# Layer A of a two-layer decoder step: an odd unit's scores and transposes in two visits of four banks, and the short chunk's scores beside the first transposes

## The chip, the cores and the metric

One core of one Trainium2 chip. The metric is device time in microseconds (us) of one execution. The kernel is one launch that computes the whole step; its program is laid out in advance, engine by engine: TensorE (PE), VectorE (DVE), ScalarE (ACT), GpSimd (POOL) and SyncE (SP), which issues nearly all DMAs.

## The reference, cut to what matters

Layer 0 is an RWKV-7 time mixing over 272 prompt tokens (16 meta tokens and 256 of the prompt) and 8 sample tokens, with 64 heads of 64. Four projections of width 4096 (r, k, v, z) feed a recurrence per head:

```python
def rwkv7_step(S, inp):
    r, d, k, v, kk, b = inp
    sa = jnp.einsum('bhij,bhj->bhi', S, kk)
    S = S * d[:, :, None, :] - sa[..., None] * b[:, :, None, :] + v[..., None] * k[:, :, None, :]
    return S, jnp.einsum('bhij,bhj->bhi', S, r)
```

Its output is normalised per head, gated with silu(z) and projected back. Layer 1 is a sliding-window attention; the change doesn't touch it.

## The kernel before, in words

**Large products.** The projections are 128x128 matmuls over 280 columns. Weights are split in two fp32r parts (`whi` by ACT at L195, `wlo` by DVE at L197), so each 128-row step takes three matmuls (L218, L219, L220). Layer A has 64 such products of 16 *pieces* each; a piece is six matmuls.

**The recurrence in chunks.** The prompt is cut in four chunks of 64 tokens and a short one of 16. A *unit* `u` is two pairs of heads, that is four heads; there are 16 units, and two of them (even, odd) make a group `o` of eight heads. For each unit `prep` and `prep_e` make `KB` (keys, one buffer for all units) and `E` (queries). Then `scores(u)` does three things:
- scores of chunks 0 and 1, of chunks 2 and 3 (`c0` 0 and 2; L1013, 8 matmuls each), and of the short chunk (L1027, 4 matmuls), each into two PSUM banks, one for each `q`. They use 64 rows and 128 columns of the array. In the profile an f32 matmul has two records, so a visit of 8 shows as x16.
- ACT copies the blocks of the triangular system out of the banks into `F` and `ND` (L1019, L1032), and DVE writes masked scores into `E` (L1020, L1021, L1033, L1034).
- transposes of `KB` for the two head pairs `j` (L1045, 10 each, one record each), which ACT copies to `BK` (L1047).

After the short chunk's scores of an odd unit, `substitute(o)` inverts the 16x16 triangular blocks of the whole group, mostly on DVE: POOL masks `ND`, a transpose to `NL` (L1065), 28 small steps in sequence (L1071, L1073), and transposes to `TN` and `TR` (L1077, L1078). `solve(o)` (L1098 to L1128, matmuls `ps_so`) joins the blocks, and `chain(o)` (matmuls `ps_ch`) runs the five chunks. `group_norm` transposes the result (`ps_yt`, L1271, read by DVE at L1272).

**What sets the order.** `drive` takes one piece of a large product, then lets every stream whose time has come put its matmuls behind it, and so on. A stream says with `yield n` how many pieces it waits before its next step; one such step is called a *visit* here. On PE this order is kept as written; DVE and ACT are ordered by a scheduler that is run when the program is built. An even unit's scores run as a side stream beside the chain of the group before; an odd unit's are part of the stream `main`: scores, `solve`, `chain`, and so on for eight groups.

**Banks.** `pm` (3 banks) takes the large products, `pe` (2 banks) the scores, the transposes and `solve`, `pp` (1) small work, and `pcy` (one tile of two banks, `two_banks`) the chain and `group_norm`. Before, an odd unit's second and fourth visits borrow `pcy` as well.

## Time and profile before

| | |
|---|---|
| three runs | median 2121.87 us (2119.55 to 2125.27) |
| profiled execution | 2132.89 us, of which span 2131.1 us |
| TensorE clock granted, mean | 0.989 |
| busy, share of the span | PE 97%, DVE 79%, ACT 59%, POOL 6% |
| from 150 to 1290 us (layer A's recurrence beside its products) | 1140 us: PE busy 1099.99, DVE 879.85, ACT 738.48 |

The profile is one execution, 11 us above the median of the runs. Times in it are counted from the span's start. "Busy" of PE counts matmuls that overlap in the array, so a busy PE can still lose time between matmuls; that is read from the starts of neighbouring matmuls.

### The profile page before, as it was taken

What the parts mean: (1) busy time and instruction counts of PE and PEld (TensorE: products, weight loads), DVE (VectorE), ACT (ScalarE), POOL (GpSimd) and SP (SyncE); (2) the same over time, 40 slices, a digit from 0 to 9 for tenths busy, and PEclk for the clock granted to TensorE, in tenths of its full rate; (3) what the DMA queues carried; (4) which work ended last, traced back from release to release, by engine and by line L of the source; (5) the groups of instructions that cost most, each with busy time, mean ns of one, the idle gap of its engine ahead of it and who ended that gap; (6) DMA issues with size and microseconds to landing.
All of it is one profiled execution on the core that took longest, in us unless ns stands there. A gap on an engine that the chain in (4) does not pass through costs nothing.

```text
span 2131.1 us, 55813 instructions
## 1 busy us (share of the span) xinstructions
PE 2073.1 (97%) x21420; PEld 1971.4 (93%) x21420; DVE 1685.4 (79%) x4080; ACT 1252.9 (59%) x2757; POOL 121.5 (6%) x188
## 2 busy tenths in 40 slices
PE   9999999899999989999999999999999999999997
PEld 7999898899899989999999999999999999999997
DVE  7866767687678768888888787987888888878885
ACT  3456666576765757767675455565565655644443
POOL 0011100001010010100100001100000000000000
PEclk9999999999999999999999999999999999999999
DMA  7997667668657766777656678757455454567774
GB/s 256 315 314 243 177 215 241 183 186 289 208 178 211 251 207 204 214 225 212 203 161 222 217 239 253 237 186 223 143 149 171 137 158 135 178 203 252 227 220 134
DMA packets 276356, 446.28 MB, mean 209 GB/s; under 512 B 54056, under 2 KB 97768, under 8 KB 275696
## 3 DMA queue, kind: packets, MB, share of 16 engines
q1 hardware_dynamic: 275656, 441.66, 66.4%
q8 instruction: 168, 2.75, 0.5%
q10 hardware_dynamic: 432, 1.05, 0.1%
q14 instruction: 100, 0.82, 0.1%
HBM read 381.69 MB, written 65.03 MB: 210 GB/s over the span
## 4 chain that ended last, share of the span: by engine, by line
PE 60%; DVE 3%; DMA 2%; issue 1%; ACT 1%; POOL 0%; POOLq 0%; DVEq 0%; SPq 0%; ACTq 0%
PE ps_z L218 6%; PE ps_z L219 5%; PE ps_z L220 5%; PE ps_ob L218 3%; PE ps_ob L220 3%; PE ps_ob L219 3%; PE ps_q L218 3%; PE ps_q L220 3%; PE ps_q L219 3%; PE ps_oa L219 2%; PE ps_oa L218 2%; PE ps_oa L220 2%; PE ps_o L218 1%; PE ps_o L219 1%; PE ps_o L220 1%
## 5 line engine op out<-in xcount | busy, mean ns | idle before, releaser
L218 PE MATMUL ps_z<-mhlm,whi_z 128*128 128x280 f32 x512 | 158.7, 310 | 0.4 <-ACT st L789 0.4
L220 PE MATMUL ps_z<-mhlm,wlo_z 128*128 128x280 f32 x512 | 149.6, 292 | 2.7 <-issue 2.7
L218 PE MATMUL ps_q<-bmh,whi_qb 128*128 128x264 f32 x512 | 150.0, 293 | 0.4 <-ACT whi_qb L195 0.3
L219 PE MATMUL ps_z<-mhlm,whi_z 128*128 128x280 f32 x512 | 149.8, 292 | 0.0
L218 PE MATMUL ps_z<-bmh,whi_zb 128*128 128x264 f32 x512 | 147.5, 288 | 0.0
L220 PE MATMUL ps_q<-bmh,wlo_qb 128*128 128x264 f32 x512 | 145.6, 284 | 0.6 <-DVE wlo_qb L197 0.6
L219 PE MATMUL ps_q<-bml,whi_qb 128*128 128x264 f32 x512 | 145.6, 284 | 0.0
L219 PE MATMUL ps_z<-bml,whi_zb 128*128 128x264 f32 x512 | 145.4, 284 | 0.0
L220 PE MATMUL ps_z<-bmh,wlo_zb 128*128 128x264 f32 x512 | 145.4, 284 | 0.0
L218 PE MATMUL ps_ob<-ghi,whi_ob 128*128 128x264 f32 x512 | 145.3, 285 | 0.0
L220 PE MATMUL ps_ob<-ghi,wlo_ob 128*128 128x264 f32 x512 | 144.6, 284 | 0.0
L219 PE MATMUL ps_ob<-glo,whi_ob 128*128 128x264 f32 x512 | 144.6, 283 | 0.0
L195 ACT CAST whi_ob<-raw_ob 128x512 fp32r<-128x512 f32 x128 | 79.1, 620 | 96.9 <-PE ps_ob L219 75.4
L195 ACT CAST whi_oa<-raw_oa 128x512 fp32r<-128x512 f32 x128 | 79.2, 620 | 89.7 <-PE ps_oa L219 27.9
L197 DVE TENSOR_TENSOR wlo_r<-raw_r,whi_r 128x512 fp32r<-128x512 f32 x128 | 87.5, 688 | 48.7 <-ACT whi_r L195 46.3
L218 PE MATMUL ps_v<-mhlm,whi_v 128*128 128x280 f32 x384 | 121.4, 316 | 0.4 <-ACT st L789 0.4
L218 PE MATMUL ps_k<-mhlm,whi_k 128*128 128x280 f32 x384 | 120.4, 313 | 1.1 <-ACT st L789 1.1
L197 DVE TENSOR_TENSOR wlo_v<-raw_v,whi_v 128x512 fp32r<-128x512 f32 x128 | 87.4, 687 | 41.0 <-ACT whi_v L195 37.8
L195 ACT CAST whi_v<-raw_v 128x512 fp32r<-128x512 f32 x128 | 79.1, 618 | 66.5 <-PE ps_v L219 39.5
L195 ACT CAST whi_zb<-raw_zb 128x512 fp32r<-128x512 f32 x128 | 78.2, 619 | 62.6 <-PE ps_z L219 39.3
L220 PE MATMUL ps_k<-mhlm,wlo_k 128*128 128x280 f32 x384 | 112.9, 294 | 1.2 <-issue 1.1
L219 PE MATMUL ps_k<-mhlm,whi_k 128*128 128x280 f32 x384 | 113.0, 294 | 0.0
(473 smaller groups left out, 7584.2 us busy)
## 6 DMA issues: line engine op xcount, KB each, us to landing
raw_k<-a_w_rkvz SPq DMA_DIRECT2D x128, 256.0 KB
raw_v<-a_w_rkvz SPq DMA_DIRECT2D x128, 256.0 KB
raw_r<-a_w_rkvz SPq DMA_DIRECT2D x128, 256.0 KB
raw_z<-a_w_rkvz SPq DMA_DIRECT2D x128, 256.0 KB
raw_oa<-a_w_out SPq DMA_DIRECT2D x128, 256.0 KB
raw_qb<-b_w_qz SPq DMA_DIRECT2D x128, 256.0 KB
raw_zb<-b_w_qz SPq DMA_DIRECT2D x128, 256.0 KB
raw_ob<-b_w_o SPq DMA_DIRECT2D x128, 256.0 KB
```

Of the source, the lines that this page charges most:

```text
L195: self.nc.scalar.copy(hi, src)
L197: return self.nc.vector.tensor_tensor(lo, src, hi.bitcast(F32), op=ALU.subtract)
L218: mm(ps, wh, xh, start=start, stop=False)
L219: mm(ps, wh, xl, start=False, stop=False)
L220: return mm(ps, wl, xh, start=False, stop=stop)
```

## The change

Visits of a unit's scores and transposes, with the pieces waited before each:

| | before | after |
|---|---|---|
| even unit | 8 c0=0; 6 c0=2; 6 short chunk; 5 transposes j=0; 4 transposes j=1 | 8 c0=0; 6 c0=2; 6 short chunk and transposes j=0; 5 transposes j=1 |
| odd unit | 8 c0=0; 3 c0=2; 4 short chunk; 3 transposes j=0; 3 transposes j=1 | 8 c0=0 and c0=2; 8 short chunk, transposes j=0 and j=1 |

The short chunk's scores take columns 0 to 63 of their two banks, and the transposes of j=0 columns 64 to 383 of the same banks. In an odd unit the second part of each visit goes to `pcy`. The copies out of the banks stand behind the whole visit; `substitute` comes behind the short chunk's copies and ahead of those of the transposes. `solve` then waits 30 pieces where it waited 24 behind the last transposes (33 and 27 from group 5 on). No matmul, copy or DMA is added or removed.

```diff
-        gap = iter((8, 3, 4, 3, 3) if odd else (8, 6, 6, 5, 4))
-        turn = iter((0, odd, 0, odd, 0))
-        def banks(nm):
-            if next(turn):
+        gap = iter((8, 8) if odd else (8, 6, 6, 5))
+        def banks(second, nm):
+            if second and odd:
...
+        def pairs(ps, c0):
+            for j in range(2):
+                for c in range(2):
+                    for q in (1, 0):
+                        o = 64 * (c0 + c)
+                        mm(ps[q][:, j, c], kb(q, j, c0 + c), rows(q, j, o, o + 64), start=True, stop=True)
...
+        def last(ps):
             for j in range(2):
                 for q in (1, 0):
+                    mm(ps[q][:, j], kb(q, j, 4), rows(q, j, 256, L), start=True, stop=True)
...
+        def turned(ps, j):
+            for c in range(5):
+                for q in (1, 0):
+                    transpose(ps[q][:, c], kb(q, j, c), self.ident[H(q), H(q)])
+
+        def turned_out(ps, j):
             for q in range(2):
                 A.copy(BK[:, j, :, H(q)], ps[q])
+
+        for c0 in (0, 2):
+            if c0 == 0 or not odd:
+                yield next(gap)
+            ps = [b.rearrange("p (a c t) -> p a c t", a=2, c=2) for b in banks(c0, f"sc{c0}_{u}")]
+            with self.pe_order():
+                pairs(ps, c0)
+            if odd:
+                two = [ps] if c0 == 0 else [*two, ps]
+            else:
+                pairs_out(ps, c0)
+        if odd:
+            for i in range(2):
+                pairs_out(two[i], 2 * i)
+
+        yield next(gap)
+        bs = banks(0, f"sc4_{u}")
+        ps = [b[:, :64].rearrange("p (a h t) -> p a h t", a=2, h=2) for b in bs]
+        bk = [[b[:, 64:384].rearrange("p (c t) -> p c t", c=5) for b in bs]]
+        with self.pe_order():
+            last(ps)
+            turned(bk[0], 0)
+        if not odd:
+            last_out(ps)
+            turned_out(bk[0], 0)
+            yield next(gap)
+        bk.append([b[:, :320].rearrange("p (c t) -> p c t", c=5) for b in banks(1, f"bk{u}")])
+        with self.pe_order():
+            turned(bk[1], 1)
+        if odd:
+            last_out(ps)
+            self.substitute(u // 2)
+            turned_out(bk[0], 0)
+        turned_out(bk[1], 1)
...
-        yield 24 if o < 5 else 27
+        yield 30 if o < 5 else 33
```

`pairs_out` and `last_out` hold the same ACT copies and DVE masks as before, in functions.

In the order rows below, names are line, operation, output and inputs, and the size of the output. Place one is PE in odd unit 7, where the scores of chunks 0 and 1 end (`ps_sc10_7`, `ps_sc00_7` before; `ps_sc0_71`, `ps_sc0_70` after). Before:

```order
L1013 MATMUL ps_sc10_7_9357<-E_7_9230,KB_1737 128x128
L1013 MATMUL ps_sc00_7_9356<-E_7_9230,KB_1737 128x128
L218 MATMUL ps_r_2560_1_9337<-mhlm0_23_0_8424,whi_r_2560_0_9293 128x280
L219 MATMUL ps_r_2560_1_9337<-mhlm0_23_0_8424,whi_r_2560_0_9293 128x280
L220 MATMUL ps_r_2560_1_9337<-mhlm0_23_0_8424,wlo_r_2560_0_9294 128x280
```

After, on the same engine at the same place:

```order
L1010 MATMUL ps_sc0_71_9256<-E_7_9141,KB_1737 128x128
L1010 MATMUL ps_sc0_70_9255<-E_7_9141,KB_1737 128x128
L1010 MATMUL ps_sc2_7_9268<-E_7_9141,KB_1737 128x128 x8
L218 MATMUL ps_r_2304_1_9076<-mhlm0_23_5_8680,whi_r_2304_10_9204 128x280
L219 MATMUL ps_r_2304_1_9076<-mhlm0_23_5_8680,whi_r_2304_10_9204 128x280
L220 MATMUL ps_r_2304_1_9076<-mhlm0_23_5_8680,wlo_r_2304_10_9205 128x280
```

The eight matmuls of chunks 2 and 3 (`ps_sc2_7`, in `pcy`) now follow directly, with no large product between.

Place two is PE in the same unit, where the short chunk's scores end before (`ps_sc14_7`, `ps_sc04_7`):

```order
L1027 MATMUL ps_sc14_7_9462<-E_7_9230,KB_1737 128x32
L1027 MATMUL ps_sc04_7_9461<-E_7_9230,KB_1737 128x32
L218 MATMUL ps_r_2560_0_9336<-mhlm0_23_4_8596,whi_r_2560_8_9422 128x280
L219 MATMUL ps_r_2560_0_9336<-mhlm0_23_4_8596,whi_r_2560_8_9422 128x280
L220 MATMUL ps_r_2560_0_9336<-mhlm0_23_4_8596,wlo_r_2560_8_9423 128x280
```

After, four score matmuls into `ps_sc4_71` and `ps_sc4_70` are followed by ten transposes into the same two banks, of which the last two stand here, and ten into `ps_bk7` (`pcy`):

```order
L1040 MATMUL ps_sc4_71_9385<-consts_78,KB_1737 128x64
L1040 MATMUL ps_sc4_70_9384<-consts_78,KB_1737 128x64
L1040 MATMUL ps_bk7_9403<-consts_78,KB_1737 128x64 x10
L218 MATMUL ps_l11_8_9488<-lt5h_1499,lhi_8_9196 128x280
L219 MATMUL ps_l11_8_9488<-lt5l_1500,lhi_8_9196 128x280
L220 MATMUL ps_l11_8_9488<-lt5h_1499,llo_8_9197 128x280
```

Three visits have become one; the next full-array matmul is one of `prep`'s (`ps_l11_8`).

Place three is ACT in the same unit, from the short chunk's copies (into `F`) to the last copy of the transposes (into `BK7`); `whi_r` and `lhi` are weight splits, the other rows `prep` of unit 8. Before:

```order
L1032 COPY F_1738<-ps_sc14_7_9462 32x2x16
L1032 COPY F_1738<-ps_sc04_7_9461 32x2x16
L195 CAST lhi_9_10386<-lraw_9_10323 96x512
L882 ACTIVATE ta8_9290<-ps_l11_8_9549,par2_408 128x280
L195 CAST whi_r_2816_2_9658<-raw_r_2816_2_9656 128x512
L901 ACTIVATE km1_8_9572<-ta8_9290,par2_408 128x280
L1047 COPY BK7_9236<-ps_bk0_7_9599 128x5x64 x2
L904 ACTIVATE ta8_9290<-ta8_9290,half_405 128x560
L195 CAST whi_r_2816_4_9682<-raw_r_2816_4_9680 128x512
L195 CAST whi_r_2816_6_9688<-raw_r_2816_6_9686 128x512
L1047 COPY BK7_9236<-ps_bk11_7_9640 128x5x64
L1047 COPY BK7_9236<-ps_bk01_7_9639 128x5x64
```

After:

```order
L1031 COPY F_1738<-ps_sc4_71_9385 32x2x16
L1031 COPY F_1738<-ps_sc4_70_9384 32x2x16
L1044 COPY BK7_9147<-ps_bk7_9403 128x5x64 x2
L1044 COPY BK7_9147<-ps_sc4_71_9385 128x5x64
L195 CAST lhi_9_10279<-lraw_9_10235 96x512
L1044 COPY BK7_9147<-ps_sc4_70_9384 128x5x64
L882 ACTIVATE ta8_9201<-ps_l11_8_9488,par2_408 128x280
```

The four copies of the transposes moved up behind the short chunk's two, with one weight split among them.

More of the change, by code (lines that the diff above doesn't have):

```diff
@@ L983, in scores @@
         odd = u % 2
-        gap = iter((8, 3, 4, 3, 3) if odd else (8, 6, 6, 5, 4))
-        turn = iter((0, odd, 0, odd, 0))
-        def banks(nm):
-            if next(turn):
-                two = self.two_banks(f"ps_{nm[0]}{nm[1]}")
+        gap = iter((8, 8) if odd else (8, 6, 6, 5))
+        def banks(second, nm):
+            if second and odd:
+                two = self.two_banks(f"ps_{nm}")
                 return [two[:, q] for q in range(2)]
-            return [self.bank(self.pe, f"ps_{nm[0]}{q}{nm[1]}") for q in range(2)]
+            return [self.bank(self.pe, f"ps_{nm}{q}") for q in range(2)]
         V, A, G = nc.vector, nc.scalar, nc.gpsimd
@@ L1002, in scores, with pairs_out @@
         bc = lambda m, *s: m.unsqueeze(1).unsqueeze(1).to_broadcast(s)
-        for c0 in (0, 2):
-            cs = slice(c0, c0 + 2)
-            yield next(gap)
-            ps = [b.rearrange("p (a c t) -> p a c t", a=2, c=2) for b in banks(("sc", f"{c0}_{u}"))]
-            with self.pe_order():
-                for j in range(2):
-                    for c in range(2):
-                        for q in (1, 0):
-                            o = 64 * (c0 + c)
-                            nc.tensor.matmul(ps[q][:, j, c], KB[H(q), j, c0 + c, 64 * q:64 * q + 128],
-                                             rows(q, j, o, o + 64), start=True, stop=True)
+        mm, transpose = nc.tensor.matmul, nc.tensor.transpose
+        kb = lambda q, j, c: KB[H(q), j, c, 64 * q:64 * q + 128]
+        def pairs(ps, c0):
[4 more added lines that the diff above has]
+                        mm(ps[q][:, j, c], kb(q, j, c0 + c), rows(q, j, o, o + 64), start=True, stop=True)
+        def pairs_out(ps, c0):
+            cs = slice(c0, c0 + 2)
             for q in range(2):
@@ L1021, in scores @@
                 tt(out(3 + q, slice(0, 128)), pv[:, :, :, 64:128], bc(self.cst(C_MASK + 64, 64), 128, 2, 2, 64), op=MU)
-        yield next(gap)
-        ps = [b[:, :64].rearrange("p (a h t) -> p a h t", a=2, h=2) for b in banks(("sc", f"4_{u}"))]
-        with self.pe_order():
+        def last(ps):
             for j in range(2):
                 for q in (1, 0):
-                    nc.tensor.matmul(ps[q][:, j], KB[H(q), j, 4, 64 * q:64 * q + 128], rows(q, j, 256, L),
-                                     start=True, stop=True)
@@ L1029, in scores @@
-        for q in range(2):
-            pv, kr = ps[q], H(1 - q)
-            r1, r2 = (slice(64 * h, 64 * h + 32) for h in (q, q ^ odd))
-            A.copy(self.ND[r2, 16 + i0 // 4:18 + i0 // 4, 0:16], pv[r1, :, 0])
-            tt(E[kr, q, :, 256:L], pv[kr, :, 0], self.cst(C_MASK, 16, kr).unsqueeze(1).to_broadcast((64, 2, 16)), op=MU)
-            tt(E[:, 3 + q, :, 256:L], pv[:, :, 1], self.cst(C_MASK + 64, 16).unsqueeze(1).to_broadcast((128, 2, 16)),
-               op=MU)
-        if odd:
-            self.substitute(u // 2)
@@ L1039, in scores, with last_out @@
-        for j in range(2):
-            yield next(gap)
-            ps = [b[:, :320].rearrange("p (c t) -> p c t", c=5) for b in banks(("bk", f"{j}_{u}"))]
-            with self.pe_order():
-                for c in range(5):
-                    for q in (1, 0):
-                        nc.tensor.transpose(ps[q][:, c], KB[H(q), j, c, 64 * q:64 * q + 128], self.ident[H(q), H(q)])
+                    mm(ps[q][:, j], kb(q, j, 4), rows(q, j, 256, L), start=True, stop=True)
+        def last_out(ps):
+            for q in range(2):
+                pv, kr = ps[q], H(1 - q)
+                r1, r2 = (slice(64 * h, 64 * h + 32) for h in (q, q ^ odd))
+                A.copy(self.ND[r2, 16 + i0 // 4:18 + i0 // 4, 0:16], pv[r1, :, 0])
+                tt(E[kr, q, :, 256:L], pv[kr, :, 0], self.cst(C_MASK, 16, kr).unsqueeze(1).to_broadcast((64, 2, 16)),
+                   op=MU)
+                tt(E[:, 3 + q, :, 256:L], pv[:, :, 1], self.cst(C_MASK + 64, 16).unsqueeze(1).to_broadcast((128, 2, 16)),
+                   op=MU)
```

## The prediction

> **What bounds the kernel now.** I read the page's engine shares and its chain of waits first, then a window over layer A's recurrence, then who PE waited for, then the timeline of PE around single visits.

> ```profile
> PE 2073.1 (97%) x21420; PEld 1971.4 (93%) x21420; DVE 1685.4 (79%) x4080; ACT 1252.9 (59%) x2757; POOL 121.5 (6%) x188
> ...
> PE 60%; DVE 3%; DMA 2%; issue 1%; ACT 1%; POOL 0%; POOLq 0%; DVEq 0%; SPq 0%; ACTq 0%
> ```

> PE is busy for 97% of the span, and the chain that ended last runs through no other engine for more than 3%. The next row is the window of layer A's recurrence (length, then busy time and instructions of PE, PEld, DVE, ACT and POOL):

> ```profile
> 150.00:1290.00 1140.00, 1099.99 (x13679) 1032.65 (x13679) 879.85 (x1984) 738.48 (x1622) 82.96 (x137) 0.99 0.69 215
> ```

> PE leaves 40 us of 1140 idle, DVE 260. So PE's own time sets the length here, and a microsecond taken from its row of matmuls is a microsecond of the run, unless a new wait takes it back. The waits that there are (total, times, longest):

> ```profile
> PE ps_yt L1271 <- DVE vT L1272: 11.0, 6, 7.3
> PE ps_so L1098 <- DVE TN L1077: 5.5, 2, 4.3
> PE ps_so L1104 <- issue: 3.3, 1, 3.3
> ```

> None is a wait of the scores or transposes for a bank. The change must therefore act on what is not idle: the price of a visit beyond its matmuls. One odd unit's five visits on PE (start, length):

> ```profile
> 218.25 1.16 PE L1013 MATMUL ps_sc<-E,KB 64*128 64x128 f32 x16
> 222.25 1.16 PE L1013 MATMUL ps_sc<-E,KB 64*128 64x128 f32 x16
> 227.04 0.64 PE L1027 MATMUL ps_sc<-E,KB 64*128 64x32 f32 x8
> 230.52 0.53 PE L1045 MATMUL ps_bk<-consts,KB 64*128 64x64 f32 x10
> 233.50 0.53 PE L1045 MATMUL ps_bk<-consts,KB 64*128 64x64 f32 x10
> ```

> **What a visit costs.** A score visit and a transpose visit with the large matmuls around them:

> ```profile
> 186.85 0.29 PE L220 MATMUL ps_r<-mhld,wlo_r 128*128 128x280 f32 x1
> 187.07 1.16 PE L1013 MATMUL ps_sc<-E,KB 64*128 64x128 f32 x16
> 188.17 0.40 PE L218 MATMUL ps_r<-mhld,whi_r 128*128 128x280 f32 x1
> 188.40 0.29 PE L219 MATMUL ps_r<-mhld,whi_r 128*128 128x280 f32 x1
> 188.53 0.29 PE L220 MATMUL ps_r<-mhld,wlo_r 128*128 128x280 f32 x1
> ...
> 204.60 0.29 PE L220 MATMUL ps_r<-mhld,wlo_r 128*128 128x280 f32 x1
> 204.82 0.53 PE L1045 MATMUL ps_bk<-consts,KB 64*128 64x64 f32 x10
> 205.28 0.40 PE L218 MATMUL ps_r<-mhld,whi_r 128*128 128x280 f32 x1
> 205.51 0.29 PE L219 MATMUL ps_r<-mhld,whi_r 128*128 128x280 f32 x1
> ```

> Large matmuls start 0.13 us apart (188.40, 188.53). From 186.85 to 188.40 there would be two such steps without the visit, so it adds 1.55 - 0.26 = 1.29 us; the transposes add 0.91 - 0.26 = 0.65. How much of that are the matmuls themselves is seen from windows that open ahead of the visit and close inside it, where the last count is the matmuls begun so far:

> ```profile
> 187.00:187.30 0.30, 0.23 (x4) 1.00 1.34 140
> 187.00:187.98 0.98, 0.91 (x16) 1.00 0.95 193
> ...
> 204.70:204.95 0.25, 0.13 (x4) 1.00 1.02 403
> 204.70:205.13 0.43, 0.31 (x10) 1.00 1.01 384
> ```

> Twelve score matmuls begin in 0.68 us, 0.057 each; six transposes in 0.18, 0.03 each. The matmuls of the visits are then 16 x 0.057 = 0.91 and 10 x 0.03 = 0.30 us, and 0.38 and 0.35 us are the price of entering and leaving the small tiles.

> **The terms.**
> - *Price of 32 visits.* An odd unit loses three: one of pair scores (0.38) and two of transposes (2 x 0.35), 1.08; eight odd units, 8.6. An even unit loses one of transposes, 0.35; eight of them, 2.8. Together 11.4 us, on PE's path. What the trace shows no example of is a second set of matmuls of the same 64x128 tile form behind a first without a large matmul between. The near bound is a score visit behind a chain visit, whose tile is 128x64:

> ```profile
> 287.99 0.29 PE L220 MATMUL ps_k<-mhlm,wlo_k 128*128 128x280 f32 x1
> 288.21 0.69 PE L1210 MATMUL ps_ch<-X,BK 128*64 128x64 f32 x16
> 288.72 0.64 PE L1213 MATMUL ps_ch<-X,E 128*64 128x64 f32 x16
> 289.29 1.16 PE L1013 MATMUL ps_sc<-E,KB 64*128 64x128 f32 x16
> 290.38 0.40 PE L218 MATMUL ps_k<-mhlm,whi_k 128*128 128x280 f32 x1
> 290.61 0.29 PE L219 MATMUL ps_k<-mhlm,whi_k 128*128 128x280 f32 x1
> ```

> From its first matmul to the second large one it takes 1.32 us, as the lone one does (187.07 to 188.40, 1.33). It saves only the step in (0.22 against 0.13) and the chain's step out (0.23 against 0.13), 0.2 us. So a merged visit saves 0.2 to 0.38 us. I take the far end: the matmuls joined here have the same tile form and alternate banks as those inside one visit do, and that is the 0.057 and 0.03 rows. [...]
> - *New neighbours.* In the order of PE, stretches of small tiles between full-array matmuls fall from 238 to 202: 32 by the visits, four because visits now come to stand beside visits of the chain. Four at 0.2: 0.8 us.
> - *`solve` waiting for `TN`.* Between the short chunk's scores and `solve` PE had 30 pieces and two transpose visits (1.3 us); now it has 30 pieces and the rest of its own visit (20 x 0.03 = 0.6), 0.7 less. The short chunk's copies may besides have to wait until the ten transposes in their banks are through (0.3 us). So `TN` is later against its reader by 0.7 to 1.0, and I take 0.8. The first group waits already: +0.8. Group 6 has this slack:

> ```profile
> 1044.26 1.11 DVE L1077 STREAM_TRANSPOSE TN<-NL 128x512 f32<-128x512 f32 x1
> ...
> 1047.75 0.43 PE L1098 MATMUL ps_so<-TN,Noff 32*32 32x16 f32 x30
> ```

> 2.4 us; in DVE's order three more weight splits and one more read of `ps_yt` stand ahead of its `TN` than before, 3 x 0.69 + 0.5 = 2.6 us by the rows below, so it waits about 2.6 + 0.8 - 2.4 = 1.0. Group 5 waits now (1.2 of the 5.5), and has three splits and `prep`'s products fewer ahead: -1.2. Sum +0.6. The long wait of `ps_yt` (7.3) stays: DVE stands then at a DMA of the key norms, ahead of the read of `ps_yt` in both orders:

> ```profile
> 380.35 0.93 DVE L897 SCALAR_TENSOR_TENSOR kk<-kT,par,kk 128x280 f32<-128x280 f32 x2 [4.76 <-DMA kk<-kr]
> ```

> - *The second visit waiting for `pcy`.* An odd unit (its two score visits on PE, and the first and last of its eight masks on DVE; the last row is the weight split):

> ```profile
> 345.71 1.16 PE L1013 MATMUL ps_sc<-E,KB 64*128 64x128 f32 x16
> 349.69 0.49 PE L1013 MATMUL ps_sc<-E,KB 64*128 64x128 f32 x4
> ...
> 347.70 0.41 DVE L1020 TENSOR_TENSOR E<-ps_sc,consts 64x256 f32<-64x256 f32 x1
> 350.56 0.42 DVE L1021 TENSOR_TENSOR E<-ps_sc,consts 128x256 f32<-128x256 f32 x1
> ...
> 357.19 0.41 DVE L1021 TENSOR_TENSOR E<-ps_sc,consts 128x256 f32<-128x256 f32 x1
> ...
> L197 DVE TENSOR_TENSOR wlo_r<-raw_r,whi_r 128x512 fp32r<-128x512 f32 x128 | 87.5, 688 | 48.7 <-ACT whi_r L195 46.3
> ```

> The second pair of chunks was drained 7.9 us after its matmuls began (349.69 to 357.60). Now it begins 0.9 us behind the first, so it is drained 8.8 us after the visit's start, or, if it queues wholly behind the first pair's masks (5.3 us), at 5.3 + 6.7 = 12.0. The transposes need the banks after this visit (2.2 us), eight pieces (48 x 0.13 = 6.2), other small visits (some 0.7) and half of the second visit (0.9): 10.0. Between no wait and 2.0 us in each of eight units; I take the earlier drain for most of them, since it is the length that was measured, and +1.0 for all eight together.
> - *Nothing.* Copies, masks and `substitute` are the same work on DVE and ACT, hidden by PE; four copies of transposes in a row hold ACT for 4 x 0.43 us by the next row, and the weight splits behind them are made some units ahead of their matmuls. Without that lead they would show as a wait of a large matmul, 1.7 us at most an odd unit.

> ```profile
> L1047 ACT COPY BK<-ps_bk x64: 403/427/462, 205.6 to 1152.9; 128x320 f32<-128x320 f32 x64
> ```
> - *Also nothing.* SP and POOL get no instruction more. Layer A's recurrence ends six pieces earlier; the products run on to the same last piece.

> Sum: -11.4 - 0.8 + 0.6 + 1.0 = -10.6 us, against 2132.9 us of the profiled execution (span 2131.1), so 2122.3 there. That execution lies 11 us above the median of the runs; from the median, 2121.9, the same step gives 2111 us.

> **The rivals.**
> 1. *A merged visit saves only the step in and out.* 36 x 0.2 = 7.2, less 1.6 of waits: 2116. The row behind the chain speaks for it; the steady 0.057 within a visit against it.
> 2. *Draining becomes the limit.* With four banks filled at once, the second visit waits the whole 2.0 us in all eight odd units: +16 + 0.6 - 12.2, 2126. From 1.5 us a unit on nothing is left of the gain. For it: DVE is 77% busy here and its masks alternate with ACT's copies in `pcy`; against it: 6.2 us of pieces lie between. [...] This trace shows no wait for a bank by these visits.
> 3. *Slower: `TN` is late for every `solve`.* DVE's chain hangs on the short chunk's copies. Two groups have no slack and the others, if all were like group 6, 2.4 us. A delay of x costs 8x - 14.4 at most; slower by 6.4 us needs 18.6, so x = 4.1 us. At 4.5 us: +21.6 - 12.2, 2131. For it: ACT has four copies more in a row there; against it: they stand behind the short chunk's two, not ahead.

> That the matmuls do not come to stand together is excluded by the order.

> **How the numbers follow.** 0.3% is 6.4 us, about what the runs' own spread (2119.55 to 2125.27) lets one tell. Forecast 0.64, rival 1 0.14, rival 2 in part or whole 0.13, rival 3 0.05, 0.04 for waits that fall otherwise in a reordered DVE queue. The forecast's own range is 2104 to 2115: the 12.2 with none of the waits, some of those of `ps_yt` and `TN` gone (up to 6 us), against 4.5 us more of them. Under 2115.5 lie the forecast and a third of rival 1: faster 0.68. The rest of rival 1 and most of rival 2 are within 0.3%: 0.24. Slower 0.08. The range reaches into rival 2, to 2121.

> **What would show it.** In the timeline an odd unit's score visit as one run of 32 matmuls, some 2.0 us long, and its second visit of 28, with 0.03 to 0.06 us a matmul across the seam; PE's busy time in layer A down by about 12 us; `ps_so` still waiting some 6 us for `TN` and no row of `ps_sc` or `ps_bk` waiting above 2 us. I am wrong if a new wait for `ps_sc`, `ps_bk` or `TN` totals 6 us or more, or if the seam costs 0.2 us.

## The result, and the profile after

The changed kernel takes 2141.81 us (median of 4 runs, 2139.39 to 2147.61) against 2123.57 us (median of 4, 2119.55 to 2127.62): a ratio of 1.009, 95% interval 1.0072 to 1.0108. It is 19 us slower, where 10.6 us faster was forecast. Its profiled execution took 2142.91 us, span 2141.1.

From the page of the changed kernel, the busy engines and the chain that ended last, then the window over layer A's recurrence:

```profile
PE 2071.6 (97%) x21420; PEld 1975.1 (92%) x21420; DVE 1690.7 (79%) x4080; ACT 1251.2 (58%) x2757; POOL 121.0 (6%) x188
...
PE 59%; DVE 4%; ACT 3%; DMA 2%; issue 1%; SPq 0%; DVEq 0%; POOLq 0%; ACTq 0%
```

```profile
150.00:1290.00 1140.00, 1088.02 (x13598) 1025.87 (x13597) 878.81 (x1976) 732.42 (x1615) 82.81 (x137) 0.98 0.68 213
```

PE's busy time in the window is 12 us lower, the number that the prediction named as a sign of success. It is no such sign: the window is fixed, and 81 instructions fewer fall into it. PE stood idle more, and the granted clock's mean went from 0.99 to 0.98.

Who PE waited for in the changed kernel (total, times, longest):

```profile
PE ps_yt L1302 <- DVE vT L1303: 8.0, 2, 7.1
...
PE ps_ch L1218 <- DVE X L1254: 4.0, 5, 1.4
PE ps_so L1129 <- DVE TN L1108: 4.0, 1, 4.0
PE ps_l L218 <- ACT cl L882: 3.6, 2, 3.0
PE ps_ch L1241 <- ACT X L1237: 3.6, 2, 3.4
PE ps_ch L1218 <- ACT X L1254: 2.9, 2, 2.4
PE ps_vt L851 <- ACT vk L853: 2.5, 2, 2.4
...
PE ps_bk L1040 <- DVE E L1020: 0.9, 2, 0.6
```

Before, the chain's largest row and the only row of these visits were:

```profile
PE ps_ch L1201 <- ACT W L1192: 2.9, 3, 2.2
...
PE ps_sc L1013 <- DVE E L1021: 1.0, 1, 1.0
```

Many waits of the chain, of `prep` (`ps_l`) and of the products' endings (`ps_vt`) for copies on ACT and DVE have come: in layer A, idle times above 0.3 us ahead of `ps_ch` make 13.4 us, where they made 5.1 before. Those for `TN` (5.5 before) and for banks have not grown. The visits themselves look as forecast (timeline of PE, unit 3 of the changed kernel):

```profile
346.00 0.29 PE L220 MATMUL ps_k<-mhlm,wlo_k 128*128 128x280 f32 x1
346.22 2.06 PE L1010 MATMUL ps_sc<-E,KB 64*128 64x128 f32 x32
348.21 0.40 PE L218 MATMUL ps_k<-mhlm,whi_k 128*128 128x280 f32 x1
348.44 0.29 PE L219 MATMUL ps_k<-mhlm,whi_k 128*128 128x280 f32 x1
...
357.62 0.64 PE L1025 MATMUL ps_sc<-E,KB 64*128 64x32 f32 x8
358.09 0.51 PE L1040 MATMUL ps_sc<-consts,KB 64*128 64x64 f32 x10
358.43 0.48 PE L1040 MATMUL ps_bk<-consts,KB 64*128 64x64 f32 x10
```

From 346.00 to 348.44 are 2.44 us; less two steps of 0.13 the visit adds 2.18, two lone ones added 2 x 1.29 = 2.58.

**An account of layer A.** For each trace I took the stretch from the first large product after 150 us to the last one of layer A (ps_r, ps_k, ps_v, ps_z, ps_o) and split its length in three: PE's idle times above 0.3 us; half of the time, outside these, in which the granted clock was 0.5; and the rest, called PE's work at full clock below. The half is an estimate: in the first profile's first stretch at 0.5 large matmuls start 0.23 us apart (172.87, 173.10), behind it 0.13 (176.03, 176.16). Each row is one execution.

| kernel | length | idle | lost to half clock | rest |
|---|---|---|---|---|
| before | 1140.6 | 38.8 | 14.9 | 1087.0 |
| before, second profile (e5) | 1135.8 | 37.7 | 9.1 | 1089.0 |
| changed | 1151.1 | 50.4 | 22.3 | 1078.4 |
| e2, odd units in two visits, old places | 1145.0 | 46.9 | 17.1 | 1081.0 |
| e8, odd units in three visits | 1126.8 | 37.6 | 6.6 | 1082.6 |
| e16, changed, odd units held | 1145.3 | 46.1 | 20.1 | 1079.1 |

The work shrank by 8.6 to 10.6 us; waits and half clock grew by more. What lies behind layer A takes 838.6 to 841.1 us in every kernel of this study. Over the timed runs the loss by the mean granted clock (span x (1 - clock)) was 17 to 19 us before and 28.4 after.

### The profile page after: what moved, and what is told of

Same layout as the page of the kernel before. It is cut to its first block, busy times and chain, and to the rows that moved or that the text cites. A ratio compares the mean times of both kernels' runs of the same rounds, so it can differ in the third digit from the quotient of the medians.

```text
span 2141.1 us, 55789 instructions
## 1 busy us (share of the span) xinstructions
PE 2071.6 (97%) x21420; PEld 1975.1 (92%) x21420; DVE 1690.7 (79%) x4080; ACT 1251.2 (58%) x2757; POOL 121.0 (6%) x188
## 4 chain that ended last, share of the span: by engine, by line
PE 59%; DVE 4%; ACT 3%; DMA 2%; issue 1%; SPq 0%; DVEq 0%; POOLq 0%; ACTq 0%
PE ps_z L218 6%; PE ps_z L219 5%; PE ps_z L220 5%; PE ps_ob L218 3%; PE ps_ob L220 3%; PE ps_ob L219 3%; PE ps_q L218 3%; PE ps_q L220 3%; PE ps_q L219 2%; PE ps_o L218 2%; PE ps_oa L219 2%; PE ps_oa L218 2%; PE ps_oa L220 2%; PE ps_o L219 1%; PE ps_o L220 1%
## 5 line engine op out<-in xcount | busy, mean ns | idle before, releaser
L218 PE MATMUL ps_z<-mhlm,whi_z 128*128 128x280 f32 x512 | 157.7, 308 | 2.0 <-ACT st L789 2.0
L218 PE MATMUL ps_q<-bmh,whi_qb 128*128 128x264 f32 x512 | 150.0, 293 | 0.1
L219 PE MATMUL ps_z<-mhlm,whi_z 128*128 128x280 f32 x512 | 149.5, 292 | 0.0
L220 PE MATMUL ps_z<-mhlm,wlo_z 128*128 128x280 f32 x512 | 149.3, 292 | 0.0
L218 PE MATMUL ps_z<-bmh,whi_zb 128*128 128x264 f32 x512 | 147.4, 288 | 0.0
L220 PE MATMUL ps_q<-bmh,wlo_qb 128*128 128x264 f32 x512 | 145.6, 284 | 0.6 <-DVE wlo_qb L197 0.6
L219 PE MATMUL ps_q<-bml,whi_qb 128*128 128x264 f32 x512 | 145.6, 284 | 0.0
L219 PE MATMUL ps_z<-bml,whi_zb 128*128 128x264 f32 x512 | 145.4, 284 | 0.0
L220 PE MATMUL ps_z<-bmh,wlo_zb 128*128 128x264 f32 x512 | 145.4, 284 | 0.0
L218 PE MATMUL ps_ob<-ghi,whi_ob 128*128 128x264 f32 x512 | 145.3, 285 | 0.0
L220 PE MATMUL ps_ob<-ghi,wlo_ob 128*128 128x264 f32 x512 | 144.6, 284 | 0.0
L219 PE MATMUL ps_ob<-glo,whi_ob 128*128 128x264 f32 x512 | 144.6, 283 | 0.0
L195 ACT CAST whi_ob<-raw_ob 128x512 fp32r<-128x512 f32 x128 | 79.0, 620 | 97.0 <-PE ps_ob L219 73.8
L195 ACT CAST whi_oa<-raw_oa 128x512 fp32r<-128x512 f32 x128 | 79.3, 621 | 92.7 <-PE ps_oa L219 29.3
L197 DVE TENSOR_TENSOR wlo_r<-raw_r,whi_r 128x512 fp32r<-128x512 f32 x128 | 88.0, 690 | 48.9 <-ACT whi_r L195 46.7
L218 PE MATMUL ps_v<-mhlm,whi_v 128*128 128x280 f32 x384 | 121.8, 317 | 1.5 <-ACT st L789 1.5
L197 DVE TENSOR_TENSOR wlo_v<-raw_v,whi_v 128x512 fp32r<-128x512 f32 x128 | 88.1, 689 | 43.1 <-ACT whi_v L195 39.6
L218 PE MATMUL ps_k<-mhlm,whi_k 128*128 128x280 f32 x384 | 119.2, 310 | 1.4 <-ACT st L789 0.9
L195 ACT CAST whi_v<-raw_v 128x512 fp32r<-128x512 f32 x128 | 79.0, 619 | 65.7 <-PE ps_v L219 36.1
L195 ACT CAST whi_zb<-raw_zb 128x512 fp32r<-128x512 f32 x128 | 78.2, 619 | 62.6 <-PE ps_z L219 39.3
L219 PE MATMUL ps_v<-mhlm,whi_v 128*128 128x280 f32 x384 | 114.0, 297 | 0.0
L220 PE MATMUL ps_v<-mhlm,wlo_v 128*128 128x280 f32 x384 | 113.7, 296 | 0.0
```

Source lines behind the costliest of these rows:

```text
L195: self.nc.scalar.copy(hi, src)
L197: return self.nc.vector.tensor_tensor(lo, src, hi.bitcast(F32), op=ALU.subtract)
L218: mm(ps, wh, xh, start=start, stop=False)
L219: mm(ps, wh, xl, start=False, stop=False)
L220: return mm(ps, wl, xh, start=False, stop=stop)
```

## The experiments

Each was timed beside the kernel before; "us" is the ratio's excess times 2122. Names e1 to e17 are used throughout.

**Is it the places or the bursts? (e1 to e4)** A *place* is the piece at which a visit stands: `solve` ends 61 pieces behind an odd unit's start before the change (the old place) and 62 after it (the new one), and an even unit's visits end at 29 and at 25. A *burst* is what joining makes on ACT and DVE: the copies of several visits in one row. The four runs take the visits of either kernel, for odd and even units apart, at chosen places. e1:

```diff
-        gap = iter((8, 8) if odd else (8, 6, 6, 5))
+        gap = iter((8, 7) if odd else (8, 6, 6, 5))
...
+        if u % 2 == 0:
+            yield 4
```

> Edit: the changed kernel with both merged visits, but with the places of the old cadence: an odd unit waits 8 and 7 pieces instead of 8 and 8, so `solve` ends 61 pieces behind the unit's start as in the kernel before and not 62, and an even unit ends four pieces later, at 29 instead of 25. Theory S (shift): the merged visits save what their price in the trace says (32 x 0.35 to 0.38 us, 11 us), and the loss comes from places: with the new cadence the chain's copies, the even scores' copies and `prep` meet on ACT and DVE, and `ps_ch`, `ps_l` and `ps_vt` wait. By S this kernel is faster than the one before by 6 to 11 us, 0.995 to 0.997. Theory B (bursts): the copies of two visits in one row on ACT and DVE are themselves what the chain waits for; by B it stays slow, +10 to +20 us, 1.005 to 1.009, and `ps_ch` waits as after the change (some 15 us against 6 before).

e2 has the gaps 8 and 7 in odd units and five visits in even ones:

> Edit: only the odd units' two visits of four banks, at the old places (8 and 7 pieces, `solve` ends at 61); even units in five visits as before. Theory S: faster by the odd units' price alone, 8 x 1.08 = 8.6 us less some waits, 0.996 to 0.998. Theory B: the four-bank visits are the bursts, so nearly the whole loss is here, +8 to +18 us, 1.004 to 1.008.

e3 joins the even units' visits alone (8, 6, 6, 5 and `yield 4` at the end):

> Edit: only the even units' short chunk joined with the first transposes, with four pieces at the end so that the unit ends at 29 as before; odd units in five visits and `solve` as before. Theory S: faster by 8 x 0.35 = 2.8 us at most, 0.998 to 1.0. Theory B: an even unit's burst lies beside the chain of the group before, so +2 to +6 us, 1.001 to 1.003.

e4 joins nothing:

```diff
-        gap = iter((8, 3, 4, 3, 3) if odd else (8, 6, 6, 5, 4))
+        gap = iter((8, 3, 5, 3, 3) if odd else (8, 6, 6, 2, 3))
```

> Edit: no visit is merged; all five visits of the kernel before, but with the places of the changed kernel: the odd unit's gaps are 8, 3, 5, 3, 3 (one piece more, `solve` ends at 62), the even unit's 8, 6, 6, 2, 3 (ends at 25 instead of 29). Theory S: the loss without the saving, so slower than the kernel before by 12 to 30 us, 1.006 to 1.014, with `ps_ch` and `ps_l` waiting as after the change. Theory B: no bursts, so no difference, -3 to +3 us.

Measured: e1 1.0042 (1.003 to 1.0054), +9 us; e2 1.0039 (1.0022 to 1.0055), +8; e3 1.0028 (1.0017 to 1.0039), +6; e4 1.0142 (1.0126 to 1.0158), +30. At the new places the joined visits (the changed kernel, +19) are 11 us faster than the five (e4), though up to 6 of these are e4's own: with its gaps of 2 and 3 `ps_bk` waits 6.0 us. At the old places the joined visits lose, so neither theory holds whole. There are two losses.

**Where the places cost (e5 to e7, e9 to e11, e14).** e5 is the kernel before:

> The kernel before, unchanged, profiled a second time. In the first profile PE waited 38.8 us in layer A (waits over 0.3 us) and lost 14.9 us there to stretches of 3.41 us or multiples in which the granted clock was 0.5, which stand behind most waits of over 1.2 us; that execution was 11 us above the median. Over its 17 timed runs the kernel's mean granted clock of 0.992 is a loss of 17 us, the profile's 0.989 one of 24.6. If half-speed stretches behind waits explain the spread between executions, this profile has the same work (1087 us of layer A without waits and lost clock), fewer stretches, and a time near 2121. If the program's runs differ in another way, the 1087 differs too.

It took 2127.59 us; its work was 1089.0, within 2 us of the first profile, and it lost less to half clock, as expected; its time stayed 5.5 us above the median. e6 changes only one gap of the kernel before, e7 only the even ones:

```diff
-        gap = iter((8, 3, 4, 3, 3) if odd else (8, 6, 6, 5, 4))
+        gap = iter((8, 3, 5, 3, 3) if odd else (8, 6, 6, 5, 4))    # e6
+        gap = iter((8, 3, 4, 3, 3) if odd else (8, 6, 6, 2, 3))    # e7
```

> Edit: the five visits of before, with one piece more between two odd visits (8, 3, 5, 3, 3), so `solve` ends at 62 pieces instead of 61 and the chain's visits stand one piece later against the even unit's; the even unit as before. Theory S1 (the one piece at `solve` makes the chain meet the even scores and `prep`): +12 to +30 us, with `ps_ch` and `ps_l` waiting some 12 and 4 us. Theory S2 (the even unit's early end does it): within 5 us of before.

> Edit: the five visits of before, with the even unit's last two gaps 2 and 3 instead of 5 and 4, so that it ends at 25 pieces instead of 29; odd units as before. Theory S1: within 5 us of before. Theory S2: +12 to +30 us. If both edits cost some 15 us each, the loss is neither place's own, and any move away from the old places costs.

e6 1.0112 (1.0092 to 1.0133), +24; e7 1.0057 (1.0041 to 1.0073), +12. In e7 half of that is its own short gaps (2 and 3): `ps_bk` waited 6.3 us against none before. e9 and e10 ask the same of the changed kernel, with one line each of e1's diff (e9 the gap of 7, e10 the `yield 4`):

> Edit: the changed kernel with odd gaps 8 and 7 instead of 8 and 8, so `solve` ends at 61 as before; the even unit still ends at 25. With e1 (61 and 29: +8 us), the changed kernel (62 and 25: +18) and the next run it makes a square of the two places. Theory S1 (the piece at `solve` is most of the loss): +8 to +12 us against before, `ps_ch` 5 to 7 us of waits. Theory S2 (the early end of the even unit costs by itself, as the 12 us of e7 say): +15 to +20. In e7 half of the cost was `ps_bk` waiting for banks with gaps of 2 and 3, which this kernel does not have; so I hold S1 likelier.

> Edit: the changed kernel with four pieces at the end of an even unit, so that it ends at 29 as before; `solve` stays at 62. Theory S1: it stays slow, +12 to +20 us against before, with `ps_ch` waiting 10 us or more. Theory S2: +8 or less.

e9 1.0035 (1.002 to 1.005), +7; e10 1.0081 (1.0064 to 1.0099), +17. So the early end of the even unit costs little here (+19 against +17, +7 against +9), and the piece at `solve` costs 8 to 12 us (e10 less e1, the changed kernel less e9). e6 and e10 have the same places, five visits against joined ones, and are 7 us apart: there the price shows in the time, and e10's work is 9.3 us less (1077.2 against 1086.5). Two kernels move what stands beside the chain along with it (e11 the even gaps to 9, 6, 6, 5, 3; e14 `prep`):

```diff
         if u:
-            yield 3
+            yield 3 if u % 2 else 4     # e14, in prep
```

> Edit: five visits everywhere; the odd unit's gaps 8, 3, 5, 3, 3 (`solve` at 62, the chain one piece later) and the even unit's visits one piece later as well (9, 6, 6, 5, 3, ending at 29), so that chain and even scores stand to each other as in the kernel before and both stand one piece later against `prep`. Theory M1 (the chain's copies queue behind the even scores' copies): back to within 6 us of before, where `solve` alone one later cost 24. Theory M2 (they queue behind `prep`'s ACT and DVE work): still +12 us or more.

> Edit: five visits everywhere; `solve` one piece later as in e6 (8, 3, 5, 3, 3), and `prep` of the even unit one piece later too (4 pieces instead of 3 at its start), so that the even unit's scores, which start eight pieces behind the later of `solve` and `prep`, the chain, and `prep` all stand to each other as in the kernel before, one piece later in a cycle that is one longer. Theory M2 (the chain's copies queue behind `prep`'s work on ACT and DVE when they stand one piece nearer to it): back to within 7 us of before, where `solve` alone cost 24 and `solve` with the even scores 15. If it stays at +12 or more, it is the place against the large products (their weight splits and their copies), which this edit does not move.

e11 1.0068 (1.0051 to 1.0085), +14; e14 1.0083 (1.0067 to 1.0098), +18. Neither goes back: my theories of the one piece, M1 and M2, fell. What e14 leaves is the place against the large products. Counting pieces in the program showed what the six slowest kernels (changed, e4, e6, e10, e11, e14) share. Start of the odd units, in pieces:

```
before, e1, e2, e3, e5, e7, e8, e9, e12, e13     70 180 299 409 519 634 747 860
changed, e4, e6, e10, e11, e14                   70 181 292 403 514 625 739 853
```

One piece more at `solve`, and `prep` of unit 5 ends at piece 290 and not 298; the third group starts 7 pieces earlier, later ones 5 to 9, against large products that stay where they are.

**The places, put back (e15, e16).** In `main`, for e6 and for the changed kernel:

```diff
-                yield 0, self.after(0, ('p', n + 1), ('c', n))
+                due, at = self.after(0, ('p', n + 1), ('c', n)), {4: 300, 10: 637}.get(n, 0)
+                yield 0, lambda: due() and self.pos >= at
```

> Counting the pieces at which the streams' steps stand in the program gives a new theory. In the kernel before, odd units start at pieces 70, 180, 299, 409, 519, 634, 747, 860; with `solve` one later (the changed kernel and e4, e6, e10, e11, e14 alike) at 70, 181, 292, 403, 514, 625, 739, 853: the third unit no longer waits for `prep` of its own unit, which ends at 290 instead of 298, so from the third group on the whole recurrence stands 6 to 9 pieces earlier against the large products, in gaps of 111 pieces where before two of them were 119 and 115. Edit: e6 (five visits, `solve` one later, +24 us) with the third odd unit held until piece 300 and the sixth until 637, so the units start at 70, 181, 300, 411, 522, 637, 751, 865. Theory H (the earlier, denser recurrence costs, not the one piece): within 7 us of before. Theory L (the one piece between `solve` and the rest of its own group costs): +12 us or more, as e6, e11 and e14.

> Edit: the changed kernel, with nothing but the third odd unit held until piece 300 and the sixth until 637 (units at 70, 181, 300, 411, 522, 637, 751, 865). Theory H: the 11 us between the changed kernel and e9 are gone, so +3 to +9 us against before, with `TN` still late and `ps_ch` waiting 5 to 8 us. Theory L: +12 to +18, as the changed kernel.

e15 0.9987 (0.9972 to 1.0001), where e6 was 1.0112; e16 1.0022 (1.0007 to 1.0036), where the changed kernel was 1.009. Theory H holds: the earlier recurrence costs some 14 us (1.009 - 1.0022; e9, with `solve` at its old place, gave 12) of the changed kernel, and a later `solve` by itself nothing. The 14 rests on the timed runs: e16's profiled execution lies 9 us above its median, and the two profiles are only 6 us apart in layer A, because `ps_so`, `ps_sm` and `ps_z` wait longer in e16's. In e16 the largest wait of the chain is 1.9 us, and `ps_ch` waits 4.2 us in idle times above 0.3 us against 13.4. What such a wait consists of, the changed kernel's PE and ACT at 964 us show:

```profile
961.68 0.46 PE L1232 MATMUL ps_ch<-W,TT 64*64 64x64 f32 x16
...
968.29 1.12 PE L1241 MATMUL ps_ch<-X,BK 128*64 128x64 f32 x16 [3.41 <-ACT X L1237]
```

```profile
962.16 0.42 ACT L915 ACTIVATE Pp<-cl 128x256 f32<-128x256 f32 x1 [0.20 <-DVE cl L909]
...
964.41 0.67 ACT L917 ACTIVATE cl<-cl 128x560 f32<-128x560 f32 x1
...
965.53 1.29 ACT L1018 COPY F<-ps_sc 32x256 f32<-32x256 f32 x4
966.84 0.62 ACT L901 ACTIVATE km<-ta,par 128x280 f32<-128x280 f32 x1
967.49 0.75 ACT L1237 COPY X<-ps_ch 64x256 f32<-64x256 f32 x2
```

The copy of the chain's X starts 5.8 us behind its matmuls (961.68 to 967.49), behind `prep`'s exponentials, a product's `st` and `th` and the even scores' copies. The same step of the kernel before (e5, PE and then ACT):

```profile
959.66 0.46 PE L1201 MATMUL ps_ch<-W,TT 64*64 64x64 f32 x16
...
962.80 0.69 PE L1210 MATMUL ps_ch<-X,BK 128*64 128x64 f32 x16
```

```profile
959.28 0.62 ACT L195 CAST whi_z<-raw_z 128x512 fp32r<-128x512 f32 x1
959.93 1.29 ACT L1019 COPY F<-ps_sc 32x256 f32<-32x256 f32 x4
961.24 0.75 ACT L1206 COPY X<-ps_ch 64x256 f32<-64x256 f32 x2
```

It starts 1.6 us behind (959.66 to 961.24), with `prep`'s pieces elsewhere; PE did not wait. Whether the phase against the large products or the denser row (gaps of 111 pieces for 119 and 115) makes such meetings, these runs do not separate.

**The loss at the old places (e8, e12).** e8 leaves the short chunk's scores by themselves and joins the rest of an odd unit:

```diff
-        gap = iter((8, 3, 4, 3, 3) if odd else (8, 6, 6, 5, 4))
-        turn = iter((0, odd, 0, odd, 0))
+        gap = iter((8, 7, 6) if odd else (8, 6, 6, 5, 4))
+        turn = iter((0, odd, 0, 0, odd))
```

(the c0 = 0 and 2 loop and the j loop wait only at their first step when `odd`, and copy behind the second).

> Edit: odd units in three visits at the old places: both pairs' scores in four banks (8), the short chunk's scores alone (7, as in the kernel before, with its copies right behind), both heads' transposes in four banks (6); `solve` and even units as before. It saves two visits of an odd unit, 8 x (0.38 + 0.35) = 5.8 us by the forecast's price, some 4.5 by the size found in the two-visit kernels. Theory T (in the two-visit kernels at the old places the short chunk's copies stand behind 20 transposes, `TN` comes 1.5 to 3 us later and `ps_so` waits 16 us instead of 10, and half-clock stretches behind those waits take the gain): here `TN` is not later, `ps_so` waits about 10 us, and the kernel is 2 to 6 us faster than before, 0.997 to 0.999. Theory R (any reordering of DVE's and ACT's queues costs about as much as it saves): +2 to +8 us, as with the two-visit odd units.

e8 0.9984 (0.997 to 0.9997), -3 us, against +8 of e2, which differs only in where the transposes stand. `TN` ended on the mean of the eight groups 27.2 us behind the first short-chunk matmul before, 27.2 in e8, 29.3 in e2. Theory T has the right place and the wrong reason: the first step on the short chunk's copies, the transpose to `NL`, starts as early in e2 (+5.6, +4.9 and +4.1 us in the first three groups) as in e8 (+4.8, +5.0, +3.9). The delay arises among the 28 steps behind it. e2, first group, ACT and then DVE:

```profile
230.13 0.76 ACT L1047 COPY BK<-ps_bk 128x320 f32<-128x320 f32 x2
230.77 0.78 ACT L1047 COPY BK<-ps_sc 128x320 f32<-128x320 f32 x2
231.41 0.65 ACT L195 CAST whi_r<-raw_r 128x512 fp32r<-128x512 f32 x1
```

```profile
232.09 1.32 DVE L197 TENSOR_TENSOR wlo_r<-raw_r,whi_r 128x512 fp32r<-128x512 f32 x1 [1.44 <-ACT whi_r L195]
...
241.54 0.69 DVE L197 TENSOR_TENSOR wlo_r<-raw_r,whi_r 128x512 fp32r<-128x512 f32 x1 [1.75 <-ACT whi_r L195]
```

The four copies of the transposes hold ACT, `whi` comes late, and DVE waits for it in its order, with `substitute`'s steps queued behind. In e8, ACT in the same group:

```profile
231.78 0.60 ACT L195 CAST whi_r<-raw_r 128x512 fp32r<-128x512 f32 x1
232.45 1.42 ACT L1066 COPY BK<-ps_bk 128x320 f32<-128x320 f32 x4
```

Here the same four copies stand in a row too, but three `whi` casts (at 228.51, 230.60 and 231.78) come between the short chunk's copies and them; in e2 none does. So it is the row's place ahead of casts that DVE needs, not the row as such. No run moves these copies alone: this is read from the traces. Between an odd unit's short-chunk matmuls and its `TN`, DVE waited for a `whi` 18.1 us in the eight groups of e2, 5.4 in e8, 7.2 in e5; the 12.7 us between e2 and e8 are most, not all, of the delay of 8 x 2.1 = 16.8.

How much of the time the late `TN` costs is not settled. PE's idle before `ps_so` is 16.3 us in e2 and 10.8 in e8, but the rows that wait for `TN` (e2, then e8) differ by 2.6 only:

```profile
PE ps_so L1201 <- DVE TN L1180: 8.3, 2, 4.2
PE ps_so L1117 <- DVE TN L1096: 5.7, 2, 3.4
```

Most of the rest stands in rows called "issue" (6.8 against 3.0), for which the profile shows no cause. Lost to half clock are 17.1 against 6.6. e12 adds to e8 the even units' joining at another place (gaps 8, 6, 11, 4):

> Edit: the three odd visits of e8 (2.7 us faster than before), and the even unit's short chunk joined with the first transposes at the transposes' old place (gaps 8, 6, 11, 4), so that no transpose moves and only the short chunk's scores of an even unit, on which `substitute` does not wait, come five pieces later. It saves 24 visits, by the measured size of the price some 6 us of PE's own time (4.4 in e8 and 1.5 more). If the places of the transposes were what made the even unit's joining cost 6 us in e3, this is 2 us faster than e8: -4 to -6 against before, 0.997 to 0.998. If any reordering costs, it is 0 to +5.

e12 0.9992 (0.998 to 1.0005): work 1081.2, 1.4 us less than e8, and no gain in time. Why an even unit's joining does not pay stays open.

**Half clock behind a wait (e13).**

```diff
+        for _ in range(28 if o == 0 else 0):
+            nc.tensor.transpose(ps[:, :128], self.ident, self.ident)
         for i in range(16):
             for q in Q:
                 nc.tensor.matmul(ps[q, 16 * i:16 * i + 16], Noff[q, i], TN[q, :, i], start=True, stop=True)
```

> Edit: the three odd visits of e8, and ahead of the first group's `solve` 28 transposes of the identity into its own bank, whose values nothing reads; by the 0.11 us from start to start of such a transpose they last 3.1 us. In every profile so far PE waits there 3 to 4 us for `TN` with nothing to do, and a stretch of half clock of 3.41 or 6.83 us follows. Theory C (half clock follows from PE having nothing to do): the stretch behind this wait is gone, the wait is under 1.2 us, `TN` comes no later, and the kernel is 1.7 to 3.4 us faster than e8, that is 3 to 6 us faster than before, 0.997 to 0.9985. Theory N (the clock falls for another reason, load or time): the stretch at some 257 us stays, and the time is that of e8.

PE at the first group's `solve`, in e8 and then in e13:

```profile
256.71 1.27 PE L1117 MATMUL ps_so<-TN,Noff 32*32 32x16 f32 x128 [3.38 <-DVE TN L1096]
257.92 0.53 PE L218 MATMUL ps_r<-mhld,whi_r 128*128 128x280 f32 x1
258.25 0.43 PE L219 MATMUL ps_r<-mhld,whi_r 128*128 128x280 f32 x1
258.48 0.43 PE L220 MATMUL ps_r<-mhld,wlo_r 128*128 128x280 f32 x1
```

```profile
253.26 3.22 PE L1116 MATMUL ps_so<-consts 128*128 128x128 f32 x28
257.00 1.27 PE L1119 MATMUL ps_so<-TN,Noff 32*32 32x16 f32 x128 [0.52 <-DVE TN L1096]
258.20 0.40 PE L218 MATMUL ps_r<-mhld,whi_r 128*128 128x280 f32 x1
258.44 0.29 PE L219 MATMUL ps_r<-mhld,whi_r 128*128 128x280 f32 x1
258.56 0.29 PE L220 MATMUL ps_r<-mhld,wlo_r 128*128 128x280 f32 x1
```

Large matmuls start 0.23 us apart behind the wait (258.25, 258.48), 0.12 where PE had been kept busy (258.44, 258.56); the granted clock from 258.00 to 261.41 us was 0.50 in e8 and 1.00 in e13. For this stretch theory C holds in the trace. The gain in time is not shown: 0.9964 (0.995 to 0.9977) is 4 us under e8's, with intervals that overlap, and over the whole of layer A e13's profile lost more to half clock than e8's (12.9 against 6.6), in stretches at other places.

**Both remedies (e17).** e13 with 21 fillers, `solve` at 25 (28 from group 5) instead of 24 (27), and e15's hold:

> What the runs point to, put together: the three odd visits of e8, the filling transposes of e13 (21 instead of 28, since `TN`'s reader comes one piece later), `solve` one piece later and the odd units held as in e15 (70, 181, 300, 411, 522, 637, 751, 865). If the gains add (-2.7 for the three visits, -4.9 more with the filling, -2.7 for later `solve` with held starts), 2112 to 2116, 0.995 to 0.997 of before. If the filling and the later `solve` buy the same wait of `TN` twice, it is that of e13, 0.9964; a new meeting of the chain with other work would make it slower than e13.

e17 0.9946 (0.9927 to 0.9965), 2111.93 us: the fastest kernel here, 11.5 us under the one before. The interval overlaps the range for gains that add (0.995 to 0.997) and holds e13's 0.9964 as well, so whether they add stays open.

## Why the prediction was wrong, step by step

- *What bounds it*: right, but incomplete. PE's path sets the length (PE 97% busy in either kernel, 60% of the chain that ended last before and 59% after); a wait of PE costs its own length and, in these traces, often half of a stretch of half clock behind it, which the prediction never priced. In the first profile that was 14.9 us in seven stretches, on 38.8 of idle.
- *Price of 32 visits*, 11.4, and *new neighbours*, 0.8: right in kind. An odd unit's joined scores add 0.40 us less than their parts (0.38 forecast), an even unit's joined visit 0.32 less (0.35), and an odd unit's second visit 0.65 less, once 0.46 (0.70); all of it is 8.6 to 10.6 us in the account, where 12.2 was forecast. Rival 1 (0.2 a visit) is out.
- *`TN`*, +0.6: the step's reasoning (path of PE 0.7 us shorter, ten transposes ahead of the copies) gave a delay of 0.8 us; at the old places it was 2.1. In the changed kernel, whose groups had moved, the wait row of `TN` fell from 5.5 to 4.0: the term came out with the other sign.
- *`pcy`*, +1.0: right, 0.9 us of `ps_bk`. The prediction's reading that no visit waited for a bank before missed one row, 1.0 us of an even unit's `ps_sc`; it is gone after, so that the net is nothing. Rival 2 is out.
- *Nothing* (copies hidden): the first step that failed. The cover it named, splits made ahead of their matmuls, holds for PE, since no product of layer A waits for a split after the change; but `wlo` waits for `whi` on DVE, and `substitute` stands behind it there. With the transposes joined to the short chunk the kernel is 11.7 us slower than with them apart (e2 less e8, 1.0039 - 0.9984). Rival 3's late `TN` did come at the old places, by 2.1 us where it needed 4.1, and by another way than the short chunk's copies.
- *Also nothing* (the recurrence ends six pieces earlier): the second, and larger. The prediction saw the six pieces in the order and took a shift against the large products as free; it is some 14 us (the changed kernel less e16), with the chain waiting for ACT and DVE.
- *The signs of being wrong* that it named did not come: no new wait for `ps_sc`, `ps_bk` or `TN` reached 6 us, and the seam of the joined scores cost nothing. They all stood at the visits themselves; the loss was elsewhere.

Sum: -9.6 of work (1078.4 against the mean of 1087.0 and 1089.0), +14.4 for the earlier recurrence (changed less e16), and +14.3 left for e16's +4.7. The 14.3 is a remainder; the 11.7 of e2 against e8 are the part that the runs tie to a step, the transposes joined to the short chunk. The even unit's joining costs 6 us alone (e3) and 1 beside the odd unit's (e1 less e2), with no cause found. None of the rivals had this.

## What to carry to other kernels

Where an order is laid out by piece counts with conditions ("when both are done"), count where every stream starts before and after an edit: one piece can tip a condition and move half of the program. Work hidden from the bounding engine need not be free: a second engine may wait for it, in its order, ahead of something that the first will need, as DVE did here for `whi` ahead of `TN` (18.1 us in the eight groups of e2). Follow the queue one engine further. And price a wait of TensorE with the half clock that may stand behind it (before: 14.9 us lost so on 38.8 us of idle).

## What the hardware showed

```profile
964.50:967.90 3.40, 0.38 (x3) 0.15 (x2) 3.35 (x9) 3.27 (x11) 0.00 (x0) 0.99 0.70 220
967.90:971.31 3.41, 3.02 (x37) 2.91 (x38) 3.40 (x8) 2.69 (x5) 0.68 (x1) 0.51 0.22 41
```

All 132 such stretches in layer A of the 19 traces at hand had PE idle for at least 1 us in the 6.8 us ahead of them. Of waits of 2 us and more 96 of 114 ended inside one or had one begin within 3.41 us behind them; of 1.6 to 2 us 21 of 50, of 1.2 to 1.6 us 22 of 89, of 0.8 to 1.2 us 8 of 119. Of the 80 waits between 2 and 3.41 us, 62 did.
